# A decoder layer whose input arrives transposed: mean squares by narrow matmuls, and twelve early blocks of the embedding product

## The chip, the core and the metric

The kernel runs on one core of one Trainium2 chip. The metric is the device time in microseconds (us). One execution was profiled; its views name the engines PE (TensorE), DVE (VectorE), ACT (ScalarE), POOL (GpSimd) and SP (SyncE, which issues all DMAs here).

## The reference

One decoder layer over x (1024 tokens by 1024 features), all in fp32:

```
h      = RMSNorm(x) * norm_mix_g
proj   = h @ w_in                     # q, k, v, z_a, gate-lowrank, four conv parts, g_a, g_c
y_a    = (headnorm(GLA(q, k, v, gk)) * silu(z_a)) @ w_branch_a
y_c    = (cb * causal_conv3(cc * xc)) * silu(z_c) @ w_branch_c
merged = sigmoid(g_a + b_ga) * y_a + sigmoid(g_c + b_gc) * y_c
x1     = x + merged @ w_out
x2     = x1 + sigmoid(RMSNorm(x1) @ w_ple_gate) * (p @ w_ple_proj)
out    = RMSNorm(x2)
```

The change touches the first line, and the product p @ w_ple_proj, whose two factors (1024 by 256 and 256 by 1024) are called p and W_pe here.

## The kernel before

**Arithmetic.** Every large product is made of fp32r matmuls on a split of each operand: `hi` is a cast (ACT) and `lo` is the operand less `hi` (DVE), function `split`, line 546. `mm3` (line 557) issues three matmuls, hi by hi, hi by lo, lo by hi. The large products use a Strassen-like scheme with seven products of half-size blocks: class `Cell` (line 661) is one output cell, and `hres[k]` is the split block k of the transposed h that product k needs. Blocks 0 and 3 come from the first 512 tokens alone; 1, 2, 4, 5 and 6 are sums and differences with the second 512.

**Order.** Nothing is issued when the code calls it. A recorder (`Flow`, line 237) notes each operation with an assumed cost; `set_dues` (line 330) works out by when each is due; `put_in_order` (line 374) simulates five engines and writes one fixed order for each. Matmuls noted with `nc.side = False` keep their order; those with `nc.side = True` are put among them as soon as the simulation says that they could run. In it a load is over 2.2 us (`LATE`, line 466) behind the end of its bytes at 340 KB per us. On the chip each engine and SP's queue work that order off and wait at the first instruction whose operand isn't there. Buffers are kept by tag and count: SBUF tag `T` has four, the PSUM banks are `m0` to `m5`, and two more banks have the tag `o`.

**The first stage** (`prep0`, lines 838 to 930). Sixteen matmuls on zeros (line 834) come first. SP loads the first 512 columns of W_pe and of p (512 KB each, line 847), `vec`, four blocks of x of 128 tokens (512 KB each), the second columns of W_pe and p, and the other four blocks of x. `pe_block` (line 880) makes one 128 by 512 block of p @ W_pe by six matmuls in bank m4 or m5, ACT copies it out and SP stores it to DRAM, to be read near the end of the kernel. Eight blocks have their place ahead of h, eight are side work. `prep_x` (line 867) takes one block of x: ACT squares it and sums each row (`junk` holds the squares, nobody reads them), POOL makes mean + EPS and its power -0.5, DVE scales the rows, PE transposes eight 128 by 128 pieces into two `o` banks, and DVE multiplies them by `gmix` into the four tiles `hq` (transposed h by quarters). `two_products` (line 897) then runs products 0 and 3 of the four cells of g_a, and later of g_c, in banks m0 to m3, and `step(k)` builds `hres[k]`.

**After it** come the products v, q, k (phase `v`, line 935, begins with v0's product 0), the attention, the convolution, the merge and the two last products, none of which the change edits.

Of the kernel before, what the change touches and what calls it, by code (L numbers as in the profile page):

```python
# [9 lines left out]
F32 = mybir.dt.float32  # L10
# [226 lines left out]
class Flow:  # L237
# [136 lines left out]
    def put_in_order(self):  # L374
# [28 lines left out]
        while len(order) < len(ops):  # L403
            best = None
            for e in range(5):
                found = [(max(clock[e], w), n) for n in waiting[e] for w in [since(ops[n])] if w is not None]
                first = None
                if e == PE and at < len(main) and not ops[main[at]].left:
                    w = since(ops[main[at]])
                    if w is not None:  # L410
                        first = (max(clock[e], w), main[at])
                when = min([w for w, _ in found + ([first] if first else [])], default=None)
                if when is None or best and best[0] <= when:
                    continue
                ripe = [n for w, n in found if w <= when]
                pick = min(ripe, key=lambda n: (ops[n].due + (6.0 if ops[n].table and ops[n].table != table else 0.0), n),
                           default=None)
                best = (when, e, first[1] if pick is None else pick)
            assert best, "nothing can run"
            when, e, n = best  # L420
            o = ops[n]
            o.start = when
            if e == PE and not o.side:
                at += 1
            else:
                waiting[e].discard(n)
            cost = o.cost
            if o.table and o.table != table:
                cost, table = cost + 1.3, o.table
            clock[e] = when + cost  # L430
            if e == SP:
                pipe = max(pipe, when + 1.6) + o.bytes / 340e3
            for s in o.succs:
                q = ops[s]
                q.ready = max(q.ready, (pipe + LATE if e == SP else when + cost + q.preds[n])
                              + (SIDE if q.engine == PE != e and q.side else 0.0))
                q.left -= 1
                if not q.left and (q.engine != PE or q.side):
                    waiting[q.engine].add(s)
            for b in o.bufs:  # L440
                if b.place is None:
                    b.place = min((w, k) for k, w in enumerate(b.tag.free) if w is not None)[1]
                    b.tag.free[b.place] = None
                    b.tag.next += 1
                b.left -= 1
                if b.pool.name == "ps":
                    b.ends[e] = when + cost
                b.until = max(b.until, pipe + LATE if e == SP else when + cost + (0.0 if e == PE and not o.side else o.lat))
                if not b.left:
                    b.tag.free[b.place] = b.until  # L450
            order.append(o)
# [12 lines left out]
SIDE = 0.5  # L464
BACKLOG = 3.0
LATE = 2.2


@with_exitstack
def kernel(  # L470
# [6 lines left out]
    wgk2: bass.AP,  # L477
    wpe: bass.AP,
    pT: bass.AP,
    vecs: bass.AP,  # L480
    gbc: bass.AP,
    tri: bass.AP,
# [8 lines left out]
    def f(ap):  # L491
        return ap.bitcast(F32)
# [18 lines left out]
    vec = cp.tile([P, 62], F32, name="vec")  # L511
    dcs = cp.tile([P, H, 2, NP, 2], F32, name="dcs")
    dds = cp.tile([P, H, 2, NP], F32, name="dds")
    junk = cp.tile([P, D], BF16, name="junk")
    bgk = vec[:, 0:4]
    bga = vec[:, 4:12]
    bgc = vec[:, 12:20]
# [311 lines left out]
    hres = [None] * 7  # L829
    zero = bp.tile([P, 512], F32R, tag="u2", name="zero", bufs=2)  # L830
    nc.vector.memset(f(zero), 0.0)
    warm = [psm.tile([P, 512], F32, tag=f"m{i}", name=f"warm{i}") for i in range(6)]
    nc.side = False
    for n in range(16):
        mm(warm[n % 6], zero[:, 0:P], zero, start=True, stop=True)
    nc.side = True

    with phase("prep0") as pool:
        pr_ = slot(4, "h", "pTraw", (2, SEQ), F32)
        wr_ = slot(4, "l", "wperaw", (2, D), F32)  # L840
        xs = [slot(1 + n // 2, "hl"[n % 2], f"x0_{n}", (2, D), F32) for n in range(4)]
        xt = [xs[st // 2][:, st % 2, :] for st in range(8)]
        halves = [slice(hh * 512, (hh + 1) * 512) for hh in range(2)]
        pre = [Cell(f"{m}{c}p", "B", W[f"{m}{c}"], hres, gate_cons(c, bias, dst), prods=(0, 3))
               for m, bias, dst in (("ga", bga, gad), ("gc", bgc, gcd)) for c in range(4)]

        load(wr_[:, :, halves[0]], wpe[:, :, halves[0]])
        load(pr_[:, :, halves[0]], pT[:, :, halves[0]])
        load(vec, vecs)
        for st in range(4):  # L850
            load(xt[st], x[rows(st), :])
        load(wr_[:, :, halves[1]], wpe[:, :, halves[1]])
        load(pr_[:, :, halves[1]], pT[:, :, halves[1]])
        for st in range(4, 8):
            load(xt[st], x[rows(st), :])
        load(trim, tri)
        pth, ptl = slot(5, "h", "pThi", (2, SEQ)), slot(5, "l", "pTlo", (2, SEQ))
        wph, wpl = slot(6, "h", "wpehi", (2, D)), slot(6, "l", "wpelo", (2, D))

        def split_half(hi, lo, src, hh):  # L860
            cs = halves[hh]
            split(hi[:, :, cs], lo[:, :, cs], src[:, :, cs])

        q = [pool.tile([P, 4, HALF], F32, name=f"hq{i}") for i in range(4)]
        quad = {(0, 0): q[0], (1, 0): q[1], (1, 1): q[2], (0, 1): q[3]}

        def prep_x(st):
            ms = sm.tile([P, 1], F32, tag="ms", name=f"ms_x{st}", bufs=4)
            act(junk, xt[st], AF.Square, scale=1.0 / 32.0, accum_out=ms)
            r = rstd_of(ms, f"r_x{st}")  # L870
            nc.vector.tensor_scalar(xt[st], xt[st], r[:, 0:1], None, op0=ALU.mult)
            for kh in range(2):
                pt = pso.tile([P, 4, P], F32, tag="o", name=f"pt_x{st}_{kh}", bufs=2)
                for k in range(4):
                    kk = 4 * kh + k
                    transpose(pt[:, k, :], xt[st][:, kk * P:(kk + 1) * P])
                tt(quad[st // 4, kh][:, :, (st % 4) * P:(st % 4 + 1) * P], pt,
                   gmix[:, 4 * kh:4 * kh + 4, None].to_broadcast([P, 4, P]), op=ALU.mult)

        def pe_block(b, c):  # L880
            acc = psm.tile([P, 512], F32, tag=f"m{4 + (b + c) % 2}", name=f"pe{b}_{c}")
            nc.side = b >= 4
            for kt in range(2):
                mm3(acc, pth[:, kt, rows(b)], ptl[:, kt, rows(b)], wph[:, kt, halves[c]],
                    wpl[:, kt, halves[c]], kt == 0, kt == 1)
            nc.side = True
            t = bp.tile([P, 512], F32, tag="T", name=f"pe{b}_{c}", bufs=4)
            nc.scalar.copy(t, acc)
            store(ped[b][:, halves[c]], t)

        hb, steps = build_a("h", q)

        def step(k):
            steps[k]()
            hres[k] = hb[k]

        def two_products(cells):
            acc = [psm.tile([P, 512], F32, tag=f"m{n}", name=f"{c.name}X") for n, c in enumerate(cells)]
            for c, X in zip(cells, acc):
                c.product(0, X, True)  # L900
                t = ev(f"{c.name}s1")
                nc.scalar.copy(t, X)
                store(s1d[pre.index(c)], t)
            for c, X in zip(cells, acc):
                c.product(3, X, False)
                c.cons(0, 0, X)

        split_half(wph, wpl, wr_, 0)
        split_half(pth, ptl, pr_, 0)
        split_half(wph, wpl, wr_, 1)  # L910
        for c in range(2):
            for b in range(4):
                pe_block(b, c)
        for st in range(4):
            prep_x(st)
        step(0)
        step(3)
        split_half(pth, ptl, pr_, 1)
        for st in range(4, 8):
            prep_x(st)  # L920
        two_products(pre[:4])
        for k in (1, 2):
            step(k)
        two_products(pre[4:])
        step(4)
        for c in range(2):
            for b in range(4, 8):
                pe_block(b, c)
        step(6)
        step(5)  # L930

# [548 lines left out]
def _lay_out(inp):  # L1480
# [17 lines left out]
    def quads(m):  # L1498
# [15 lines left out]
        "wgk2": np.concatenate([a["w_gk2"][0]] * 8),  # L1514
        "wpe": a["w_ple_proj"][0].reshape(2, 128, 1024).transpose(1, 0, 2),
        "pT": a["p"][0, 0].T.reshape(2, 128, 1024).transpose(1, 0, 2),
        "vecs": vecs,
        "gbc": np.broadcast_to(a["norm_final_g"], (128, 1024)),
        "tri": np.triu(np.ones((128, 128), np.int32)),
# [21 lines left out]
```

## Time and profile before

| what | value |
|---|---|
| three runs, us | 1123.02, 1125.8, 1123.91 |
| their median, us | 1123.91 |
| the profiled execution, us | 1124.92 |
| its span, first to last instruction, us | 1123.1 |
| mean granted TensorE clock | 0.997 |

A row of the timeline has the start in us from the span's beginning, the length in us, the engine, the line (459 is the planner's one call, so operations are told apart by their tiles), the instruction, output<-inputs, partitions x elements, and the count of merged instructions; in brackets stands the idle time ahead of it and what ended it. `PEld` is PE's load of the stationary operand. A row of one tile's instructions has the count and the shortest, median and longest duration in ns, then the first and last start. In the table of stretches the numbers behind a stretch's length are busy us with the count of instructions for PE, PEld, DVE, ACT and POOL, then the granted clock, the DMA engines' busy share, and GB/s.

### The profile page before, as it was taken

To read this page: it belongs to the slowest core of one execution; us is meant where nothing else is said; L and a number is where in the kernel's file an instruction comes from. 1 tells how busy PE (TensorE), PEld (TensorE's weight loads), DVE (VectorE), ACT (ScalarE), POOL (GpSimd) and SP (SyncE) were. 2 spreads that over 40 slices of the span, in tenths; PEclk is the share of its full clock that TensorE was granted. 3 is DMA by queue.
4 is the path that set the end of the run, shared out by engine and by line. 5 is a ranking of instruction groups with operands and counts; after the bars stand their busy time and mean duration, and the time that the engine had idled before them with its cause. 6 is when DMAs were issued, how large, how long until landed. Compare 5 with 4: busy or idle time off the path is not lost. (4 is left out here: it accounts for less than half of the span.)

```text
span 1123.1 us, 15414 instructions
## 1 busy us (share of the span) xinstructions
PE 1104.9 (98%) x5132; PEld 915.3 (81%) x5132; DVE 858.3 (76%) x1370; ACT 585.4 (52%) x1089; POOL 72.2 (6%) x131
## 2 busy tenths in 40 slices
PE   8999999999999999999999999999999999999996
PEld 7788888888888888888888888888888887787884
DVE  6986776988785856757748677776999879879675
ACT  7766765654443333333343376766736444457553
POOL 1200000000000000000000022220000000102031
PEclk9999999999999999999999999999999999999998
DMA  9844466987993122121212599998594888787853
GB/s 345 273 169 142 133 194 190 276 237 264 318 328 126 57 86 65 55 94 46 94 56 69 192 292 307 348 294 293 207 317 162 288 260 291 274 273 267 285 192 126
DMA packets 154207, 232.66 MB, mean 207 GB/s; under 512 B 12304, under 2 KB 74000, under 8 KB 151056
## 3 DMA queue, kind: packets, MB, share of 16 engines
q1 hardware_dynamic: 154128, 231.68, 62.1%
q8 instruction: 40, 0.66, 0.2%
q14 instruction: 39, 0.32, 0.1%
HBM read 154.04 MB, written 77.59 MB: 206 GB/s over the span
## 5 line engine op out<-in xcount | busy, mean ns | idle before, releaser
L459 ACT ACTIVATE junk<-x 128x512 bf16<-128x512 f32 (+1 forms) x40 | 28.6, 716 | 23.5 <-DVE x L459 19.1
L459 POOL MEMSET t<- 128x2 f32 x8 | 0.8, 100 | 471.5 <-DVE u L459 271.0
L459 POOL TENSOR_SCALAR rg<-ms 128x1 f32<-128x1 f32 x8 | 8.0, 1003 | 260.9 <-ACT junk L459 260.9
L459 DVE TENSOR_TENSOR wt<-wt 128x512 f32<-128x512 f32 x32 | 21.8, 686 | 2.1 <-DMA szd<-sz 0.8
L459 DVE SCALAR_TENSOR_TENSOR u<-t,vec,u 128x1024 f32<-128x1024 f32 x16 | 20.5, 1278 | 0.0
L459 POOL TENSOR_TENSOR or<-or,mhalf 128x1 f32<-128x1 f32 x32 | 19.7, 618 | 2.6
L459 DVE COPY_PREDICATED aT<-trim,X 128x128 f32<-128x128 int32 x32 | 9.6, 300 | 11.0 <-PE X L459 8.3
L459 ACT ACTIVATE og<-op,or 128x256 f32<-128x256 f32 x32 | 15.1, 472 | 5.1 <-POOL or L459 3.6
L459 POOL TENSOR_SCALAR or<-oms 128x1 f32<-128x1 f32 x32 | 9.8, 305 | 124.1 <-ACT junk L459 123.9
L459 DVE TENSOR_TENSOR oT<-op,szl 128x256 f32<-128x256 f32 x32 | 13.4, 420 | 5.6 <-ACT junk L459 2.9
L459 DVE TENSOR_TENSOR vlo<-pt_v,vhi 128x512 fp32r<-128x512 f32 x16 | 11.0, 687 | 7.0 <-ACT vhi L459 6.9
L459 ACT ACT_TABLE_LOAD x12 | 15.4, 1283 | 0.9 <-PEq L1530 0.7
L459 ACT ACTIVATE junk<-op 128x256 bf16<-128x256 f32 x32 | 12.2, 382 | 6.9 <-PE op L459 6.2
L459 PE MATMUL op<-Sh,qkl 128*128 128x256 f32 x56 | 14.7, 283 | 0.0
L459 POOL TENSOR_SCALAR rf<-ms 128x1 f32<-128x1 f32 x8 | 10.4, 1295 | 65.3 <-ACT junk L459 65.2
L459 ACT CAST vhi<-pt_v 128x512 fp32r<-128x512 f32 x16 | 9.2, 584 | 9.7 <-PE pt_v L459 8.5
L459 PE MATMUL pe<-wpehi,pThi 128*128 128x512 f32 x32 | 13.3, 415 | 0.7 <-ACT pe L459 0.7
L459 PE MATMUL op<-vl,aTh 128*128 128x256 f32 x64 | 13.9, 290 | 0.0
L459 DVE SCALAR_TENSOR_TENSOR x<-x,rf,gfin 128x1024 f32<-128x1024 f32 x8 | 10.3, 1282 | 4.2 <-POOL rf L459 4.2
L459 ACT CAST aTh<-aT 128x128 fp32r<-128x128 f32 x32 | 9.5, 297 | 7.2 <-DVE aT L459 6.9
L459 DVE TENSOR_TENSOR Sl<-S,Sh 128x256 fp32r<-128x256 f32 x28 | 11.8, 421 | 1.6 <-ACT Sh L459 1.3
L459 PE MATMUL pe<-wpehi,pTlo 128*128 128x512 f32 x32 | 12.9, 404 | 0.0
(3213 smaller groups left out, 4191.8 us busy)
## 6 DMA issues: line engine op xcount, KB each, us to landing
qkl<-qkd SPq DMA_DIRECT2D x32, 320.0 KB, 5.0
x<-in_x_dram SPq DMA_DIRECT2D x16, 512.0 KB, 5.9
wt<-in_wb_dram SPq DMA_DIRECT2D x8, 1024.0 KB, 7.7
wtd<-wt SPq DMA_DIRECT2D x32, 256.0 KB, 4.7
vl<-vd SPq DMA_DIRECT2D x32, 256.0 KB, 5.0
uq<-ud SPq DMA_DIRECT2D x5, 1024.0 KB, 5.2
oq<-od SPq DMA_DIRECT2D x5, 1024.0 KB, 6.7
ped<-pe SPq DMA_DIRECT2D x16, 256.0 KB, 3.1
```

What stands on the lines that cost most here:

```text
L459: o.call(*[place(a) for a in o.args], **{k: place(a) for k, a in o.kw.items()})
```

## The change

The host also hands over x transposed (`xT`, 128 x 8 x 1024). It is loaded straight into the four `hq` tiles, in loads of two 128-feature pieces by 512 tokens (512 KB). Nothing is transposed but the reciprocal root: `scale_h(i)`, for each 512 tokens, squares the eight pieces on ACT, adds them up pairwise on DVE, sums over the features by eight fp32 matmuls against a column of ones (two for each 128 tokens), adds EPS on DVE, takes the power on POOL for four columns at once, spreads it over 128 columns on DVE, transposes that by four PE transposes, and scales the eight pieces on DVE by `gmix` and the transposed root.

The sixteen warm-up matmuls are seven. p and W_pe are loaded in pieces of 256 KB and split piece by piece; the two second-column pieces of W_pe now come ahead of x. Twelve blocks of p @ W_pe have their place ahead of h (tokens 0 to 511 by both column halves, tokens 512 to 1023 by the first), over banks m0 to m5 in turn; the first four run all their first halves of the contraction, then the second ones. Blocks of odd number are copied out by DVE instead of ACT. Four blocks remain as side work. In the simulation a load issued in its first 30 us is over 0.8 us behind its bytes instead of 2.2.

```diff
-                q.ready = max(q.ready, (pipe + LATE if e == SP else when + cost + q.preds[n])
+                q.ready = max(q.ready, (pipe + (LATE if when > START else 0.8) if e == SP else when + cost + q.preds[n])
...
+START = 30.0
...
-    junk = cp.tile([P, D], BF16, name="junk")
+    junk = cp.tile([P, 512], BF16, name="junk")
...
-    for n in range(16):
+    for n in range(7):
         mm(warm[n % 6], zero[:, 0:P], zero, start=True, stop=True)
...
+        def get_x(i):
+            for n in (0, 3) if i == 0 else (1, 2):
+                for kp in range(0, 4, 2):
+                    kk = 4 * quad[n][1] + kp
+                    load(q[n][:, kp:kp + 2, :], xT[:, kk:kk + 2, halves[i]])
+
+        for kt in range(2):
+            load(pr_[:, kt, halves[0]], pT[:, kt, halves[0]])
+            load(wr_[:, kt, halves[0]], wpe[:, kt, halves[0]])
+        for kt in range(2):
+            load(wr_[:, kt, halves[1]], wpe[:, kt, halves[1]])
+        get_x(0)
+        load(vec, vecs)
+        for kt in range(2):
+            load(pr_[:, kt, halves[1]], pT[:, kt, halves[1]])
+        get_x(1)
...
+        def scale_h(i):
+            both = (0, 3) if i == 0 else (1, 2)
+            acc = slot(1, "hl"[i], f"sq{i}", (4, 512), F32)
+            for j, (n, kp) in enumerate((n, kp) for n in both for kp in (0, 2)):
+                d = acc[:, 0:2, :] if j == 0 else acc[:, 2:4, :] if j % 2 else slot(2, "hl"[i], f"sr{i}", (4, 512), F32)[:, 0:2, :]
+                act(d, q[n][:, kp:kp + 2, :], AF.Square, scale=1.0 / 32.0)
+                if j:
+                    tt(acc[:, 0:2, :], acc[:, 0:2, :], d, op=ALU.add)
+            sums = pso.tile([P, 4, P], F32, tag="o", name=f"ms{i}", bufs=2)
+            for s in range(4):
+                for kt in range(2):
+                    mm(sums[:, s, 0:1], acc[:, kt, s * P:(s + 1) * P], ones, start=kt == 0, stop=kt == 1)
+            r = sm.tile([P, 4], F32, tag="rx", name=f"r_x{i}", bufs=2)
+            nc.vector.tensor_scalar(r, sums[:, :, 0], EPS, None, op0=ALU.add)
+            nc.gpsimd.tensor_tensor(r, r, mhalf[:, 0:1].to_broadcast([P, 4]), op=ALU.pow)
+            rb = bp.tile([P, 4, P], F32, tag="u2", name=f"rb{i}", bufs=2)
+            nc.vector.tensor_copy(rb, r[:, :, None].to_broadcast([P, 4, P]))
+            rt = pso.tile([P, 4, P], F32, tag="o", name=f"rt{i}", bufs=2)
+            for s in range(4):
+                transpose(rt[:, s, :], rb[:, s, :])
+            rt = rt.rearrange("p s t -> p (s t)")
+            for n in both:
+                for k in range(4):
+                    kk = 4 * quad[n][1] + k
+                    stt(q[n][:, k, :], q[n][:, k, :], gmix[:, kk:kk + 1], rt, op0=ALU.mult, op1=ALU.mult)
+
+        BANKS = (0, 1, 2, 3, 4, 5, 0, 1, 2, 3, 4, 5)
+
+        def pe_blocks(bs, c, by_kt=False):
...
+                nc.side = at[0] > len(BANKS)
...
+                    (nc.vector.tensor_copy if b % 2 else nc.scalar.copy)(t, acc[b - bs[0]])
+                    store(ped[b][:, halves[c]], t)
...
-        split_half(wph, wpl, wr_, 0)
-        split_half(pth, ptl, pr_, 0)
+        for kt in range(2):
+            split(pth[:, kt, halves[0]], ptl[:, kt, halves[0]], pr_[:, kt, halves[0]])
+            split(wph[:, kt, halves[0]], wpl[:, kt, halves[0]], wr_[:, kt, halves[0]])
+        pe_blocks(range(0, 4), 0, True)
         split_half(wph, wpl, wr_, 1)
-        for c in range(2):
-            for b in range(4):
-                pe_block(b, c)
-        for st in range(4):
-            prep_x(st)
+        pe_blocks(range(0, 4), 1)
+        split_half(pth, ptl, pr_, 1)
+        pe_blocks(range(4, 8), 0)
+        scale_h(0)
         step(0)
         step(3)
-        split_half(pth, ptl, pr_, 1)
-        for st in range(4, 8):
-            prep_x(st)
         two_products(pre[:4])
+        scale_h(1)
         for k in (1, 2):
             step(k)
         two_products(pre[4:])
         step(4)
-        for c in range(2):
-            for b in range(4, 8):
-                pe_block(b, c)
+        pe_blocks(range(4, 8), 1)
         step(6)
         step(5)
```

More of the change, by code (lines that the diff above doesn't have):

```diff
@@ L447, in put_in_order @@
                     b.ends[e] = when + cost
-                b.until = max(b.until, pipe + LATE if e == SP else when + cost + (0.0 if e == PE and not o.side else o.lat))
+                b.until = max(b.until, pipe + (LATE if when > START else 0.8) if e == SP else when + cost + (0.0 if e == PE and not o.side else o.lat))
                 if not b.left:
@@ L479 @@
     pT: bass.AP,
+    xT: bass.AP,
     vecs: bass.AP,
@@ L831 @@
     nc.vector.memset(f(zero), 0.0)
+    ones = sm.tile([P, 1], F32, name="ones")
+    nc.gpsimd.memset(ones, 1.0)
     warm = [psm.tile([P, 512], F32, tag=f"m{i}", name=f"warm{i}") for i in range(6)]
     nc.side = False
-    for n in range(16):
+    for n in range(7):
         mm(warm[n % 6], zero[:, 0:P], zero, start=True, stop=True)
@@ L840 @@
         wr_ = slot(4, "l", "wperaw", (2, D), F32)
-        xs = [slot(1 + n // 2, "hl"[n % 2], f"x0_{n}", (2, D), F32) for n in range(4)]
-        xt = [xs[st // 2][:, st % 2, :] for st in range(8)]
         halves = [slice(hh * 512, (hh + 1) * 512) for hh in range(2)]
@@ L845 @@
                for m, bias, dst in (("ga", bga, gad), ("gc", bgc, gcd)) for c in range(4)]
-        load(wr_[:, :, halves[0]], wpe[:, :, halves[0]])
-        load(pr_[:, :, halves[0]], pT[:, :, halves[0]])
-        load(vec, vecs)
-        for st in range(4):
-            load(xt[st], x[rows(st), :])
-        load(wr_[:, :, halves[1]], wpe[:, :, halves[1]])
-        load(pr_[:, :, halves[1]], pT[:, :, halves[1]])
-        for st in range(4, 8):
-            load(xt[st], x[rows(st), :])
-        load(trim, tri)
+        q = [pool.tile([P, 4, HALF], F32, name=f"hq{i}") for i in range(4)]
@@ L857 @@
+        quad = [(0, 0), (1, 0), (1, 1), (0, 1)]
         pth, ptl = slot(5, "h", "pThi", (2, SEQ)), slot(5, "l", "pTlo", (2, SEQ))
         wph, wpl = slot(6, "h", "wpehi", (2, D)), slot(6, "l", "wpelo", (2, D))
-        def split_half(hi, lo, src, hh):
[L861 to L873, printed above, removed]
-                for k in range(4):
[L875 to L884, printed above, removed]
-                    wpl[:, kt, halves[c]], kt == 0, kt == 1)
[L886 to L889, printed above, removed]
+        def get_x(i):
[3 more added lines that the diff above has]
+                    load(q[n][:, kp:kp + 2, :], xT[:, kk:kk + 2, halves[i]])
@@ new lines @@
+        for kt in range(2):
[8 more added lines that the diff above has]
+        get_x(1)
+        load(trim, tri)
+        def split_half(hi, lo, src, hh):
+            for kt in range(2):
+                cs = halves[hh]
+                split(hi[:, kt, cs], lo[:, kt, cs], src[:, kt, cs])
@@ new lines @@
+        at = [0]
+        BANKS = (0, 1, 2, 3, 4, 5, 0, 1, 2, 3, 4, 5)
+        def pe_blocks(bs, c, by_kt=False):
+            acc = []
+            for b in bs:
+                n = BANKS[at[0]] if at[0] < len(BANKS) else 4 + at[0] % 2
+                acc.append(psm.tile([P, 512], F32, tag=f"m{n}", name=f"pe{b}_{c}"))
+                at[0] += 1
+            todo = [(b, kt) for kt in range(2) for b in bs] if by_kt else [(b, kt) for b in bs for kt in range(2)]
+            for b, kt in todo:
+                nc.side = at[0] > len(BANKS)
+                mm3(acc[b - bs[0]], pth[:, kt, rows(b)], ptl[:, kt, rows(b)], wph[:, kt, halves[c]],
+                    wpl[:, kt, halves[c]], kt == 0, kt == 1)
+                nc.side = True
+                if kt == 1:
+                    t = bp.tile([P, 512], F32, tag="T", name=f"pe{b}_{c}", bufs=4)
+                    (nc.vector.tensor_copy if b % 2 else nc.scalar.copy)(t, acc[b - bs[0]])
+                    store(ped[b][:, halves[c]], t)
@@ L906, in two_products @@
                 c.cons(0, 0, X)
-        split_half(wph, wpl, wr_, 0)
-        split_half(pth, ptl, pr_, 0)
+        for kt in range(2):
+            split(pth[:, kt, halves[0]], ptl[:, kt, halves[0]], pr_[:, kt, halves[0]])
+            split(wph[:, kt, halves[0]], wpl[:, kt, halves[0]], wr_[:, kt, halves[0]])
+        pe_blocks(range(0, 4), 0, True)
         split_half(wph, wpl, wr_, 1)
-        for c in range(2):
-            for b in range(4):
-                pe_block(b, c)
-        for st in range(4):
-            prep_x(st)
+        pe_blocks(range(0, 4), 1)
+        split_half(pth, ptl, pr_, 1)
+        pe_blocks(range(4, 8), 0)
+        scale_h(0)
         step(0)
         step(3)
-        split_half(pth, ptl, pr_, 1)
-        for st in range(4, 8):
-            prep_x(st)
         two_products(pre[:4])
+        scale_h(1)
         for k in (1, 2):
@@ L1516, in _lay_out @@
         "pT": a["p"][0, 0].T.reshape(2, 128, 1024).transpose(1, 0, 2),
+        "xT": a["x"][0].T.reshape(8, 128, 1024).transpose(1, 0, 2),
         "vecs": vecs,
```

## The prediction

> **What bounds the kernel now.** The first part of the profile, the busy time of each engine, says who is the bound; the table of stretches then says where that engine is not full.
>
> ```profile
> span 1123.1 us, 15414 instructions
> PE 1104.9 (98%) x5132; PEld 915.3 (81%) x5132; DVE 858.3 (76%) x1370; ACT 585.4 (52%) x1089; POOL 72.2 (6%) x131
> ```
> ```profile
> 0.00:100.00 100.00, 96.38 (x435) 77.33 (x436) 75.41 (x105) 70.78 (x115) 13.12 (x25) 1.00 0.68 236
> 100.00:200.00 100.00, 100.00 (x470) 82.05 (x469) 71.87 (x112) 60.04 (x97) 0.00 (x0) 1.00 0.59 179
> 1000.00:1123.10 123.10, 110.15 (x500) 90.32 (x498) 93.96 (x132) 66.00 (x124) 23.10 (x24) 0.97 0.65 226
> ```
>
> PE is the first number behind each stretch's length. It has a matmul running 98% of the span, all of 100 to 200 us, and its only large holes are in the last 123 us, which the change leaves alone. So the time is PE's list of matmuls plus its holes, and a microsecond won or lost before 100 us is carried to the end, since PE works its list off in order. The question is what the first 60 us of PE hold. Its waits up to 130 us, and its timeline, whose first column is the start:
>
> ```profile
> PE ga0pX L459 <- DVE h0lo L459: 0.8, 1, 0.8
> PE pe L459 <- ACT pe L459: 0.7, 1, 0.7
> PE pt_x L459 <- DVE hq L459: 0.6, 1, 0.6
> ```
> ```profile
> 8.02 0.39 PE L459 MATMUL pe<-wpehi,pThi 128*128 128x512 f32 x1
> 8.25 0.39 PE L459 MATMUL pe<-wpelo,pThi 128*128 128x512 f32 x1
> ...
> 10.65 0.39 PE L459 MATMUL pe<-wpehi,pTlo 128*128 128x512 f32 x1
> 11.73 0.50 PE L459 MATMUL pe<-wpehi,pThi 128*128 128x512 f32 x1 [0.70 <-ACT pe L459]
> ...
> 14.06 1.03 PE L459 MATMUL pt_x<-ident,x 128*128 128x128 f32 x8
> 14.85 0.48 PE L459 MATMUL pe<-wpehi,pThi 128*128 128x512 f32 x1
> 15.16 0.40 PE L459 MATMUL pe<-wpelo,pThi 128*128 128x512 f32 x1
> ...
> 23.86 0.39 PE L459 MATMUL ga0pX<-h0hi,ga0phi 128*128 128x512 f32 x1
> 25.09 0.50 PE L459 MATMUL ga0pX<-h0lo,ga0phi 128*128 128x512 f32 x1 [0.84 <-DVE h0lo L459]
> ...
> 32.07 0.39 PE L459 MATMUL ga2pX<-h0lo,ga2phi 128*128 128x512 f32 x1
> 32.52 1.07 PE L459 MATMUL pt_x<-ident,x 128*128 128x128 f32 x8
> ...
> 33.89 0.40 PE L459 MATMUL ga2pX<-h0lo,ga2phi 128*128 128x512 f32 x1
> 34.84 0.66 PE L459 MATMUL pt_x<-ident,x 128*128 128x128 f32 x4 [0.56 <-DVE hq L459]
> ```
>
> Starts are read, not durations, because matmuls overlap: 8.02 to 8.25 is 0.23 us a matmul. So four things can be won: the real work begins at 8.02; eight transposes of x cost 14.85 - 14.06 = 0.79 and another 0.08 at the change back (15.16 - 14.85 - 0.23), 0.87 in all, so the 64 cost about 6.9; and the holes are 0.85 (10.88 to 11.73), 1.0 (24.09 to 25.09), 0.2 (32.30 to 32.52) and 0.7 (34.12 to 34.84), 2.8 together.
>
> **The change part by part.** *The start.* What has to arrive first, and x's first half:
>
> ```profile
> 4.65 1.04 ACT L459 CAST wpehi<-wperaw 128x1024 fp32r<-128x1024 f32 x1 [2.65 <-DMA wperaw<-in_wpe_dram]
> ...
> 6.11 1.04 ACT L459 CAST pThi<-pTraw 128x1024 fp32r<-128x1024 f32 x1 [0.42 <-DMA pTraw<-in_pT_dram]
> ```
> ```profile
> 4.94 0.94 SPq L459 DMA_DIRECT2D x<-in_x_dram  x1
> ...
> 8.74 0.33 SPq L459 DMA_DIRECT2D ga2praw<-in_wc_dram  x1
> ```
> ```profile
> DMA to landing us min/median/max: 5.3/6.7/9.1
> ```
> ```profile
> L459 DVE TENSOR_TENSOR wpelo<-wperaw,wpehi x2: 1226/1226/1227, 5.7 to 9.8; 128x1024 fp32r<-128x1024 f32 x2
> L459 DVE TENSOR_TENSOR ga0plo<-ga0praw,ga0phi x2: 680/684/687, 17.8 to 23.2; 128x512 fp32r<-128x512 f32 x2
> L459 DVE TENSOR_SCALAR x<-x,r_x x8: 745/750/756, 12.2 to 40.5; 128x1024 f32<-128x1024 f32 x8
> L459 DVE TENSOR_TENSOR hq<-pt_x,vec x16: 679/684/692, 14.7 to 43.6; 128x512 f32<-128x512 f32 x16
> ```
>
> Half a megabyte lands every 1.46 us (4.65, 6.11), so quarters land near 3.9 and 4.65. ACT then casts w's quarter (about 0.55, half of 1.04) until 5.25, DVE takes 0.68 for the remainder: PE runs steadily from about 6.05. That is -2.0. The four extra load issues cost SP 0.33 each; SP reaches the fourth x load near 5 us, as now (4.94), behind the same 1.5 MB of p and W and 1.5 MB of x, so I let it land as now, at 4.94 + 9.1 = 14.0. The planner's new 0.8 behind a load is no work; it puts the first half megabyte at 0.72 + 1.6 + 1.54 + 0.8 = 4.66 against 4.65 above, so I price it at nothing.
>
> *The clock.* Nine warm-up matmuls go.
>
> ```profile
> L459 PE MATMUL warm<-zero x16: 395/628/796, 1.4 to 7.8; 128*128 128x512 f32 x16
> ```
>
> Sixteen starts from 1.4 to 7.8 are 0.42 us apart on the mean, near double the 0.23 of the work behind them: PE runs at half pace for about its first 6 us, though the granted clock reads 1.00. Seven end near 4.6, and 6.05 comes after more than a microsecond with hardly a matmul. If the 6 us count from 1.4 all the same, PE is slow until 7.3 and loses half of 1.25, 0.6; if they count anew, until 12, and it loses 3.0. The stream is broken, so I take a value nearer the upper end: +2.0.
>
> The Trainium skill, "TensorE: Matmul & The Clock Gate", Part 1, speaks against the change here: the gate opens only after a busy window of about 3.4 us whose phase is not tied to the kernel, so a gap can spoil a window. An estimate by that page alone is a loss of 1.7 to 3.4 us, and a sum of -4.3 to -2.6 instead of the -4.0 below; the slow first 6 us agree with it, and no row here shows a gap before the clock is up.
>
> *The sums.* 64 transposes go (-6.9), 8 of the broadcast root come (+0.9). Sixteen narrow fp32 matmuls are added. The nearest row is the fp32 score product: line 1190 issues it 32 times and the trace holds 64, two passes each.
>
> ```profile
> 646.08 0.39 PE L459 MATMUL ga1Y<-h2hi,ga1lo 128*128 128x512 f32 x1
> 646.31 0.38 PE L459 MATMUL X<-qkl 128*128 128x128 f32 x2
> 646.53 0.27 PE L459 MATMUL X<-ident,qkl 128*128 128x128 f32 x1
> ```
>
> Two passes take 0.22, so 32 take 3.5, and 3.6 with the changes to and fro. Below, the loads of weights set a floor by the transposes' pace (0.79 / 8 = 0.10, 3.2); above, a full matmul's 0.23 would give 7.4. I take 3.6, since the score product also loads 128 fp32 columns per pass.
>
> *The holes.* The 0.85 goes: six banks and an alternation of ACT and DVE replace two banks behind one ACT copy. The 0.2 and 0.7 stood at x's transposes. The 1.0 before h0 depends on who is later. PE: 6.05, 72 matmuls x 0.23 = 16.6, half the sums 1.8, four transposes 0.5, clock 2.0: 26.9. The chain to h0: x at 14.0, its Square 1.06, an add 1.23, eight sums 1.8, the root, its broadcast about 0.7, transposes 0.4, two scalings 1.3, cast 1.04, remainder 1.23, and some 1.2 for nine handovers. The root is POOL's:
>
> ```profile
> L459 POOL TENSOR_SCALAR r_x<-ms_x x8: 221/461/3433, 11.3 to 38.0; 128x1 f32<-128x1 f32 x8
> L459 POOL TENSOR_TENSOR r_x<-r_x,mhalf x8: 567/567/901, 11.6 to 38.8; 128x1 f32<-128x1 f32 x8
> ```
>
> One pow of one column takes 0.57; four columns lie between 0.57 and 2.3, and I take 0.6. The chain then ends near 24.6, two microseconds ahead of PE. So -2.8 of old holes, and +1.2 of new ones for the second half's sums and transposes, which stand in PE's fixed order among the gate products, and for h0's second chunk. The bounds for the new ones are 0 and the rivals below.
>
> *The rest.* DVE loses eight scalings (8 x 0.75) and gains six adds (6 x 1.23), eight copies out of PSUM (about 0.68 each, by the row from pt_x) and two small steps a half (1.8): +8.6. The sixteen scalings that replace the reads of pt_x have the same shape. ACT loses those copies and eight accumulator reads. This hides: the last remainder of h, and the first product that needs any of the later ones, stand far apart.
>
> ```profile
> 65.08 2.36 DVE L459 TENSOR_TENSOR h6lo<-hq,h6hi 128x1024 fp32r<-128x1024 f32 x2
> ```
> ```profile
> L459 PE MATMUL v0X<-h0hi,v0hi x4: 389/389/389, 89.1 to 91.1; 128*128 128x512 f32 x4
> ```
>
> From 67 to 89 us there are 22 us of cover; were it gone, at most 8.6 would show. Four more blocks' stores (1 MB) fall before h0, and SP holds each until its copy is done; what stands behind them on SP is second-half x and gate weights, which have until 26 us. The shorter junk tile costs nothing.
>
> Sum: -2.0 - 6.9 + 0.9 + 3.6 + 2.0 - 2.8 + 1.2 = -4.0 us. Against the profiled execution (1124.92, a span of 1123.1 and 1.8 around it) that is 1120.9; that execution lies 1.0 above the median of 1123.91, against which it is 1119.9.
>
> **The rivals.** *The clock is up early and the chain never shows.* Cold loss 0.6 and no new hole: -6.6, 1117.3. For it: the planner's order gives the chain two microseconds. Against it: the gap after seven warm-up matmuls.
>
> *The narrow matmuls cost a full matmul's pace per pass*: 3.8 more, -0.2, 1123.7. Against it: 0.11 a pass in the score product.
>
> *The root is late.* POOL's 3.43 above is a step of 0.22 that could not finish while DVE ran one two-input subtraction after another; the pow has DVE's splits beside it too. With 2.9 on each half and x's last quarter 2 us later behind gate weights, h0 is ready at 29.5, PE waits 2.6 there and 2.9 in the second half, in place of 1.2: +0.3, 1124.2. "SBUF — State Buffer" of the Trainium skill, in "Who interferes with whom", gives this as a lock: a DVE instruction with two SBUF inputs shuts out a GpSimd one that reads SBUF; the 3.43 agrees.
>
> *Slower: PE stands in its own fixed order behind the chain.* The sums and the root's transposes are put among matmuls that could run. If POOL is shut out (2.9) and DVE also has a queue of splits and copies before broadcast and scaling (three at 0.68, 2.0), each half is 4.9 late at PE: 9.8 in place of 1.2, +4.6, 1128.5. It is slower by over 0.3% from 4.3 us of lateness per half. For it: before h0 DVE has eight splits, six copies, four scalings and two gate remainders at 0.68, three adds and a remainder at 1.23, some 18.5 us of work between 5 and 26 us. Against it: the slow clock delays PE by 2.0 and the chain by nothing.
>
> *The clock counts anew after the gap*: a loss of 3.0 instead of 2.0, -3.0, 1120.9. For it: no row shows the pace rising over a gap. Against it: the gap is short beside the 6 us. The page on the clock gate above has this rule, with a window in place of a count.
>
> *The quarters land no sooner than the halves*, so the work starts near 7 instead of 6.05: -3.0, 1120.9. Against it: the landings above are in proportion to the bytes.
>
> **How the numbers follow.** A measurement of this kernel can tell about 0.3%, 3.4 us, from no change; the marks are 1120.5 and 1127.3. My case, between -5.5 and -3.4, 0.38; early clock 0.17; clock anew 0.10, late root 0.11, expensive sums 0.08 and late quarters 0.05, all between -3.4 and +3.4, together 0.34; slower 0.11. So faster 0.55, same 0.34, slower 0.11. The likeliest gives 1119.9. The range reaches from 1116.0, just below the early clock, to 1124.6, a little over the late root; the slower case and a little at the lower end stay out.
>
> **What would show it.** Right: the first pe matmul before 6.2; matmuls 0.42 apart until 9 to 12 us; two passes of about 0.11 per narrow matmul; h0's first product at 26 to 28 us with under 0.5 us of wait; v0's first product 4 us earlier than 89.1. Wrong: a wait of PE at rt, ms or h0lo of over 2 us; a POOL pow of over 2 us; holes past 60 us that the kernel did not have.

## The result, and the profile after

The changed kernel takes 1139.91 us (median of four, 1138.01 to 1143.24) against 1124.4 of the kernel before beside it. The ratio is 1.0131, 95% interval 1.0110 to 1.0151: **slower by 15.5 us**, where 4.0 us less was forecast. The profiled execution is the one of 1143.24.

The head of its page, to set beside the same two lines of before:

```profile
span 1141.5 us, 15326 instructions
PE 1123.5 (98%) x5099; PEld 917.4 (80%) x5099; DVE 868.9 (76%) x1384; ACT 581.2 (51%) x1077; POOL 60.8 (5%) x118
```

PE has 33 matmuls fewer (5099 against 5132), is as full as before (98%), and yet its busy time has grown by 18.6 us. So it does not wait longer; the same matmuls take longer. The table of stretches, PE alone, shows where. First before, then after:

```profile
200.00:400.00 200.00, 200.00 (x884) 1.00 0.69 223
400.00:600.00 200.00, 200.00 (x884) 1.00 0.23 73
```
```profile
10.00:20.00 10.00, 7.29 (x25) 0.80 1.04 381
20.00:30.00 10.00, 10.00 (x36) 0.51 0.54 160
30.00:40.00 10.00, 10.00 (x46) 1.00 0.75 278
...
200.00:400.00 200.00, 200.00 (x866) 1.00 0.70 225
400.00:600.00 200.00, 200.00 (x865) 1.00 0.21 69
```

Behind PE's count stand the granted clock, the DMA share and GB/s. Between 400 and 600 us PE is full in both kernels, both have the whole clock, and the DMA engines are four fifths idle; still 865 matmuls fit in where 884 did. No line of that stage was edited. From the starts in the trace: between 250 and 600 us one 128x512 matmul follows the other after 226.67 ns before (always 226 or 227) and after 231.59 ns now (224 to 237). Over the whole program some 4,290 such steps (those under 0.3 us), 4.2 ns longer on the mean, are **18 us**.

The second thing is in the first 30 us of PE's timeline after:

```profile
1.44 3.35 PE L459 MATMUL warm<-zero 128*128 128x512 f32 x7 [1.44 <-DVE zero L459]
5.36 0.79 PE L459 MATMUL pe<-wpehi,pThi 128*128 128x512 f32 x1 [0.57 <-ACT pThi L459]
5.95 0.63 PE L459 MATMUL pe<-wpelo,pThi 128*128 128x512 f32 x1
...
8.94 0.55 PE L459 MATMUL pe<-wpehi,pTlo 128*128 128x512 f32 x1
9.33 0.40 PE L459 MATMUL pe<-wpehi,pThi 128*128 128x512 f32 x1
9.56 0.39 PE L459 MATMUL pe<-wpelo,pThi 128*128 128x512 f32 x1
...
13.19 0.39 PE L459 MATMUL pe<-wpehi,pTlo 128*128 128x512 f32 x1
15.12 0.50 PE L459 MATMUL pe<-wpehi,pThi 128*128 128x512 f32 x1 [1.54 <-ACT wpehi L459]
16.79 0.80 PE L459 MATMUL pe<-wpelo,pThi 128*128 128x512 f32 x1 [1.16 <-DVE wpelo L459]
17.38 0.63 PE L459 MATMUL pe<-wpehi,pTlo 128*128 128x512 f32 x1
17.80 0.63 PE L459 MATMUL pe<-wpehi,pThi 128*128 128x512 f32 x1
...
29.33 0.81 PE L459 MATMUL rt<-ident,rb 128*128 128x128 f32 x4
29.89 0.48 PE L459 MATMUL pe<-wpelo,pThi 128*128 128x512 f32 x1
```

Real work begins at 5.36 and is steady from 5.95. The steps are 0.43 us until 9.3 and 0.23 from there: the clock is up. At 13.19 PE runs out of work, because W_pe's second columns are not there; a wait of 1.54 for their cast and one of 1.16 for their remainder follow, and behind them the steps are 0.43 again until 29.7 (the granted clock of 20 to 30 us is 0.51): 12.9 us at half pace, 6.4 us lost in this execution. The others fared better: four executions have 1143.2, 1141.4, 1138.0 and 1138.4 us at mean clocks of 0.991, 0.993, 0.996 and 0.996. From the rise at 9.3 to the rise at 29.7 are 20.4 us. The Trainium skill, "TensorE: Matmul & The Clock Gate", Part 1, has the clock set by windows of about 3.4 us that run free of the kernel. 20.4 is 6.0 of them, so the trace agrees, as far as one interval can.

Why the work was not there, SP's issues behind the first one of p and the first two of W_pe tell (start, length):

```profile
2.10 0.43 SPq L459 DMA_DIRECT2D pTraw<-in_pT_dram  x1
2.57 0.43 SPq L459 DMA_DIRECT2D hq<-in_xT_dram  x1
3.05 0.47 SPq L459 DMA_DIRECT2D wperaw<-in_wpe_dram  x1
3.56 0.95 SPq L459 DMA_DIRECT2D hq<-in_xT_dram  x2
4.55 1.13 SPq L459 DMA_DIRECT2D wperaw<-in_wpe_dram  x1
```

The code notes the two second-column pieces of W_pe ahead of x. The planner, which sends the load that is due first, put half a megabyte of x ahead of the first piece and another megabyte ahead of the second.

What the first reading could not show is the cause of the slower steps. One candidate is not in any view: **the memory that the program gives its tiles**. The edit adds a tile of 4 bytes (`ones`), moves `mhalf` in the order of first use, and replaces eight small tiles of x's rows (32 bytes each, so 256 together) by two. In the built program every split operand of a matmul, the fourteen residents (`h`, `u`, `o`, ...) and the sixteen tiles of the weight ring (`whi`, `wlo`), starts at 160 past a multiple of 256 bytes before the change, by the accident that the small tiles between them come to 256 bytes. After it, residents start at 160, 192 or 224 past, and of the ring fourteen tiles at 224 and two at 192. Below, the place of a tile is this remainder of its start address by 256 bytes. In these products a resident is the moving operand, whose 512 columns go through PE, and a tile of the ring is the stationary one, which PE loads ahead.

### The profile page after: what moved, and what is told of

The parts are those of the page before. It is cut to its first block, busy times and chain, and to the rows that moved or that the text cites. A ratio compares the mean times of both kernels' runs of the same rounds, so it can differ in the third digit from the quotient of the medians.

```text
span 1141.5 us, 15326 instructions
## 1 busy us (share of the span) xinstructions
PE 1123.5 (98%) x5099; PEld 917.4 (80%) x5099; DVE 868.9 (76%) x1384; ACT 581.2 (51%) x1077; POOL 60.8 (5%) x118
## 5 line engine op out<-in xcount | busy, mean ns | idle before, releaser
L459 ACT ACTIVATE junk<-x 128x512 bf16<-128x512 f32 x32 | 20.1, 629 | 22.5 <-DVE x L459 18.4
L459 DVE COPY_PREDICATED aT<-trim,X 128x128 f32<-128x128 int32 x32 | 9.6, 300 | 10.6 <-PE X L459 8.1
L459 PE MATMUL pe<-wpelo,pThi 128*128 128x512 f32 x32 | 15.3, 477 | 1.2 <-DVE wpelo L459 1.2
L459 PEld LDWEIGHTS X<-qkl 128*128 128x128 f32 x64 | 11.3, 188 | 2.5 <-DMA qkl<-qkd 0.7
```

The lines of the kernel that those rows point to most:

```text
L459: o.call(*[place(a) for a in o.args], **{k: place(a) for k, a in o.kw.items()})
```

## The experiments

Theory A: the step from one matmul to the next goes by the start addresses of its operands. Theory B, the rival: it comes from the new order, the banks, the transposed load or the DMAs. Beside these, theory C on the start: the two pieces of W_pe behind x cost their waits and the clock. When the first four were written I took the grain of A to be 64 bytes; that was wrong. Each ratio below is to the kernel before, run beside that experiment; across experiments the ratios compare better than the times.

**Whole 64-byte steps for every tile, and a mixture put into the kernel before.**

```diff
-        b = Buffer(self, self.tags[tag], size, dtype, name or tag)
+        b = Buffer(self, self.tags[tag], -(-size // 16) * 16, dtype, name or tag)
```

The first is the changed kernel with this line.

> The changed kernel with every small tile rounded up to 64 bytes, so that all tiles start at a multiple of 64 bytes; nothing else differs. Theory A (addresses): the changed kernel's extra 4- and 16-byte tiles put the operands of the matmuls at two different offsets within 64 bytes (0 and 32), and matmul starts went from 227 to 231 ns apart for it; here the pace is 227 ns again and the time is 1118 to 1124 us. Rival B (the pace follows from the new order of work or from traffic): pace stays at 231 ns, time 1138 to 1143 us. Rival C (the loss lies in the first 40 us, in PE's waits and slow clock): time also stays at 1138 to 1143 us, since those are not touched.

Measured: 1138.16 us, ratio 1.0115 (1.0093 to 1.0138), steps of 231.9 ns. Nothing gained. The operands were at 0 and at 64 past 256 now, one resident at 192. The second is the kernel before with two residents 32 bytes longer, which leaves 160, 192 and 224:

```diff
-        b = Buffer(self, self.tags[tag], size, dtype, name or tag)
+        b = Buffer(self, self.tags[tag], size + (8 if tag in ("r6l", "r0h") else 0), dtype, name or tag)
```

> The kernel before, with two resident tiles (W_pe's remainder, later block 6, and block 0's cast) 32 bytes longer, so that of the matmul operands some start at 0 and some at 32 within 64 bytes; all work and its order are that of before. Theory A (addresses): pace 230 to 233 ns instead of 227, time 1137 to 1147 us. Rivals B and C: no change, 1123 to 1126 us.

Measured: 1144.12 us, ratio 1.0178 (1.0154 to 1.0201). Its table of stretches, PE alone:

```profile
200.00:400.00 200.00, 200.00 (x864) 1.00 0.69 226
400.00:600.00 200.00, 200.00 (x864) 1.00 0.20 69
```

The old order, banks and loads, and the new pace: 64 bytes of memory alone cost 20 us. So theory B is not needed for a slow pace; that it has no part in the changed kernel's is shown by the run with one place, below. The grain of 64 fell in the run ahead of this one. A third kept all residents at a multiple of 64 and the ring 32 past one, by 32 bytes more behind ten tiles, so that places within 256 bytes were mixed among both (the smallest tiles are left out of the 64-byte steps here):

```diff
+EXTRA = {'raw_2': 8, 'raw_8': 8, 'raw_9': 8, 'whi_4': 8, 'r0l_0': 8, 'whi_7': 8, 'r3h_0': 8, 'wlo_3': 8, 'r3l_0': 8, 'wlo_7': 8}
...
+            self.size += EXTRA.get(spot, 0)
```

> The changed kernel with all moving operands (the residents) at 0 within 64 bytes and all stationary ones (the ring of hi and lo pieces) at 32. Theory A1 (the two operands of a matmul must share the offset): pace 231 ns or more, time 1135 to 1145 us. Theory A2 (each stream must keep its own offset from matmul to matmul, whatever the other has): pace 227 ns, 1118 to 1124 us.

Measured: 1143.55 us, ratio 1.0170 (1.0142 to 1.0198), 232.7 ns: slow too. What before had and none of these had is one and the same place within 256 bytes for all.

**W_pe's pieces at the head of SP's queue**, in the kernel with 64-byte steps:

```diff
             load(wr_[:, kt, halves[1]], wpe[:, kt, halves[1]])
+            nc.early.append(nc.ops[-1])
...
+        for o in self.early:
+            o.due = -1e3
```

> The changed kernel with 64-byte tiles, and the two second-column pieces of W_pe issued as early as they can be, ahead of x. Theory: in the changed kernel PE idled 3.1 us for these pieces (13.4 to 16.8 us) and the clock fell back to half until 29.7; with them early the idle goes, the clock stays up, and the time is 2 to 6 us below that of the run with 64-byte tiles alone, 1114 to 1119 us. Rival: x, which then lands later, takes it back at the sums (PE waits at ms or at rt): within 1 us of the run with 64-byte tiles alone.

Measured: 1139.95 us, 1.0133 (1.0114 to 1.0152), no gain. The due time was too early: both pieces went ahead of p's first columns, and PE's waits became

```profile
PE pe L461 <- ACT pThi L461: 3.4, 1, 3.4
...
PE ga0pX L461 <- DVE h0lo L461: 1.2, 1, 1.2
```

The wait was moved, not removed; the run says nothing on theory C.

**One place in 256 bytes.** The changed kernel with two of its small tiles at 256 bytes: with `ones` at 32, every resident and every tile of the ring is at 160 again.

```diff
-        b = Buffer(self, self.tags[tag], size, dtype, name or tag)
+        b = Buffer(self, self.tags[tag], 64 if tag in ("mhalf", "rx") else size, dtype, name or tag)
```

> The changed kernel, with two small tiles (the -0.5 of the root and the two of the scales) enlarged to 256 bytes, so that every resident factor and every tile of the ring starts 160 bytes past a multiple of 256 again, as in the kernel before; order and work as in the changed kernel. Theory (the pace of the matmuls goes by the start addresses of both operands, and is best where all share one place in 256 bytes): pace from 231.6 back to 226.7 ns between 250 and 600 us, 4394 x 4.2 ns = 18.5 us less than the changed kernel, 1121 us, and less where the clock's fall in the start stage does not happen. Rival (the pace comes from the new order, the fewer banks or the transposed load, and addresses play a part only in the other test): 231 ns and 1140 us as changed.

Measured: **1119.65 us**, ratio to before 0.9951 (0.9933 to 0.9968).

```profile
10.00:20.00 10.00, 6.93 (x26) 0.83 1.06 399
20.00:30.00 10.00, 10.00 (x52) 1.00 0.77 253
...
200.00:400.00 200.00, 200.00 (x884) 1.00 0.68 220
400.00:600.00 200.00, 200.00 (x884) 1.00 0.23 71
```

884 matmuls again, 226.67 ns, and 20.3 us less than the changed kernel, of which 18.5 are the steps (4,290 times 4.3 ns). All 5099 matmuls come in the same order in both kernels, and banks and loads are kept, so theory B has nothing left to explain. The clock, for the rest, fell for 3.4 us in this execution instead of 12.9 (0.83 in the second ten us, 1.00 in the third).

The same with 128 bytes instead of 256, so that operands stand at 32 or at 160:

```diff
-        b = Buffer(self, self.tags[tag], 64 if tag in ("mhalf", "rx") else size, dtype, name or tag)
+        b = Buffer(self, self.tags[tag], 32 if tag in ("mhalf", "rx") else size, dtype, name or tag)
```

> As the kernel with the same addresses, but the small tiles enlarged to 128 bytes instead of 256: the operands start at 32 or at 160 past a multiple of 256 (two thirds at 32), all at 32 past a multiple of 128. If places are told apart within 128 bytes: 226.7 ns and the same time as with equal places. If within 256: some 230 ns or more and 12 to 18 us slower than with equal places.

Measured: 1132.51 us, 1.0072 (1.0051 to 1.0092), 230.25 ns. A shared place in 128 bytes does not do. One in 256 does: in the kernel ahead of this one the operands still lie at 1696, 1952, 160 and 416 past a multiple of 2048.

**Which difference counts: between the two operands, or from one matmul to the next?** For this the memory was set out on purpose: all residents first, then the ring, then the rest. The start was taken from the kernel with W_pe first (below).

```diff
+    def lay(self, order):
...
+        resident = [b for b in spots if b.tag.name[0] == "r" and b.tag.name[1].isdigit()]
+        ring = [b for b in spots if b.tag.name in ("whi", "wlo")]
+        for group, lead in ((resident, 0), (ring, 0)):
+            if lead:
+                group[0].pool.opened().tile([P, lead], F32, tag="lead" + group[0].tag.name, name="lead", bufs=1)
+            for b in group:
+                b.get()
...
-            for o in self.put_in_order():
+            order = self.put_in_order()
+            self.lay(order)
+            for o in order:
```

> As the kernel with the same addresses and W_pe's loads ahead of x, but the memory is set out on purpose: first the fourteen residents, then the sixteen tiles of the ring, all at 128 past a multiple of 256 (a multiple of 64), the rest behind them. Theory (only that the two operands share a place in 256 bytes counts): 226.7 ns between 250 and 600 us, 1118 us as there. Rival (160 is a place of its own, or the neighbours in memory matter): 229 ns or more, 1128 us or more.

Measured: 1118.63 us, 0.9917 (0.9895 to 0.9939), 226.67 ns: 128 is as good a place as 160. Then the ring was moved as a whole, by 128 bytes, with as much less for `mhalf`, so that most tiles behind stay put; and in the same way by 64 (16 and 48 in place of 32 and 32) and by 32 (8 and 56):

```diff
-        for group, lead in ((resident, 0), (ring, 0)):
+        for group, lead in ((resident, 0), (ring, 32)):
...
-        b = Buffer(self, self.tags[tag], 64 if tag in ("mhalf", "rx") else size, dtype, name or tag)
+        b = Buffer(self, self.tags[tag], 32 if tag == "mhalf" else 64 if tag == "rx" else size, dtype, name or tag)
```

> As the kernel set out on purpose, with the sixteen tiles of the ring 128 bytes further on: residents all at 128 past a multiple of 256, ring all at 0, so that from one matmul to the next nothing changes place, but the two operands of each matmul stand 128 bytes apart. Theory (the operands of one matmul must share a place): 230 to 233 ns, 12 to 25 us slower than set out alike. Rival (only a change of place from one matmul to the next costs): 226.7 ns and no slower.

> The same with the ring 64 bytes further on (residents at 128, ring at 192). Theory (operands of one matmul must share a place): 230 to 233 ns. If the distance sets the price: less than at 128 bytes. Rival (only changes cost): 226.7 ns.

> The same with the ring 32 bytes further on (residents at 128, ring at 160), the distance that most products of the changed kernel have (192 and 224). Theory (operands of one matmul must share a place within 256 bytes, 32 bytes being enough to part them): 230 to 234 ns, 12 to 26 us slower than set out alike. Rival (32 bytes are one place, 64 or 128 are not): 226.7 ns, 1118 us.

Measured: 1139.71 us (1.0105, 1.0085 to 1.0124), 1144.17 (one execution) and 1142.96 (1.0161, 1.0144 to 1.0178). The table of stretches of the four, 400 to 600 us, set out alike first, then 128, 64 and 32 bytes apart:

```profile
400.00:600.00 200.00, 200.00 (x884) 1.00 0.21 71
```
```profile
400.00:600.00 200.00, 200.00 (x863) 1.00 0.21 70
```
```profile
400.00:600.00 200.00, 200.00 (x859) 1.00 0.21 70
```
```profile
400.00:600.00 200.00, 200.00 (x859) 1.00 0.21 70
```

The steps are 226.67, 232.38, 233.33 and 233.33 ns. In these three nothing changes place from one product to the next; only the moving operand (a resident) and the stationary one (a tile of the ring) differ. So it is the moving and the stationary operand that must share their place, and the price is 21 to 27 us here (1.0105 and 1.0161 against 0.9917; for the ring 64 bytes on, with its one execution, 1144.17 less 1118.63). Which stationary operand is open: PE loads the next matmul's while one runs (in the kernel with one place the matmul of 300.25 us is loaded from 300.02, when the one ahead of it starts), and with a ring at one place these runs can't tell a matmul's own from the next one's.

The traces of three kernels that mix places (the changed one, the one with 64-byte steps, the one with 128 bytes) bear this out inside one execution. The program's places, put beside the matmuls of 60 to 1000 us one by one, give the step where a matmul and six on each side are alike. Where all operands are at one place it is 226.9, 227.6 and 227.3 ns (159, 156 and 160 steps); where the two operands of none share a place, 232.5, 232.5 and 232.7. Where the two always share one, but it changes among the thirteen, it is 229.7, 228.4 and 227.7 (84, 78 and 78 steps): a change seems to cost something too, but no run was made for it. Why the hardware does this is not shown by these runs.

**The start.** Equal places, and the pieces of W_pe just behind the first four quarters:

```diff
+        n = self.early[0]
+        for o in self.ops[n:n + 2]:
+            o.due = max(q.due for q in self.ops[n - 4:n]) + 1e-3
...
+        nc.early = [len(nc.ops)]
         for kt in range(2):
             load(wr_[:, kt, halves[1]], wpe[:, kt, halves[1]])
```

> The same addresses, and the two loads of W_pe's second columns issued right behind the first four quarters, ahead of the first load of x. Theory (those two loads behind x hold TensorE 1.5 and 1.2 us, and these holes let the clock fall): no wait over 1 us at the pieces of W_pe, no fall of the clock behind 10 us, 3 to 10 us less than the kernel with the same addresses alone. Rival (x, 0.5 MB or 1.5 us later, then holds h's first product by as much): the same time within 1 us, with the wait at the split of h instead.

Measured: 1118.18 us, 0.9936 (0.9921 to 0.9951), 1.5 less than with equal places alone, where 3 to 10 were expected, and the two intervals overlap. PE's waits of the first 40 us, equal places alone and then with W_pe first:

```profile
PE pe L459 <- ACT wpehi L459: 1.9, 1, 1.9
PE warm L459 <- DVE zero L459: 1.4, 1, 1.4
PE pe L459 <- DVE wpelo L459: 1.2, 1, 1.2
PE pe L459 <- ACT pThi L459: 0.5, 1, 0.5
```
```profile
PE warm L462 <- DVE zero L462: 1.4, 1, 1.4
PE ga0pX L462 <- DVE h0lo L462: 0.9, 1, 0.9
PE ga0pX L462 <- ACT h0hi L462: 0.3, 1, 0.3
PE pe L462 <- ACT pThi L462: 0.2, 1, 0.2
```

The 3.1 us at W_pe are gone, 1.2 come at h instead, and the clock does not fall (1.00 in all stretches up to 1000 us). In the two profiled executions v0's first product starts 2.6 us earlier (78.3 against 80.9). The executions also lie closer: 1116.3 to 1118.9 at a mean clock of 0.997 in all six, against 1116.7 to 1124.5 at 0.990 to 0.997 in seven. So theory C holds in the profile for the waits, and the clocks speak for its other half; but its worth in time can't be told from nothing here. Nor do these waits always bring the clock down. In the profile of the run with 64-byte steps they are there too (1.0 and 1.2 us, the second ending at 15.32), and the clock stays up behind them:

```profile
10.00:20.00 10.00, 7.87 (x42) 1.00 1.06 403
20.00:30.00 10.00, 10.00 (x47) 1.00 0.92 305
```

With sixteen warm-up matmuls in place of seven on top of that:

```diff
-    for n in range(7):
+    for n in range(16):
         mm(warm[n % 6], zero[:, 0:P], zero, start=True, stop=True)
```

> As the kernel before this one, with the sixteen warm-up matmuls of the kernel before instead of seven. Theory (the cut warm-up brings the first product 2.0 us forward, and the clock goes by a grid of windows that more warm-up reaches no sooner): 2 us slower than with seven. Rival (seven leave the first window too empty, so that the clock comes up late or falls): the clock is up earlier, and 1 to 5 us faster than with seven.

Measured: 1117.4 us, 0.9930 (0.9916 to 0.9944): no difference from seven that can be told. Its timeline shows both sides:

```profile
1.44 5.64 PE L462 MATMUL warm<-zero 128*128 128x512 f32 x16 [1.44 <-DVE zero L462]
6.91 0.39 PE L462 MATMUL pe<-wpehi,pThi 128*128 128x512 f32 x1
7.14 0.39 PE L462 MATMUL pe<-wpelo,pThi 128*128 128x512 f32 x1
```

The first product is 1.9 us later than with seven (5.00), and v0's first product only 0.9 (79.2).

## Why the prediction was wrong, step by step

**The step that failed** is the one that carried the rest of the program over unchanged: "a microsecond won or lost before 100 us is carried to the end", with "The shorter junk tile costs nothing" and not a word on the other small tiles. The sum has a term for all that the edit issues and none for what it places. That term is +18 us of longer steps against the kernel before. Between the changed kernel and the one with equal places it is 18.5 of the 20.3 us in the medians; for the other 1.8 the clock is the likeliest cause, not shown by itself. None of the rivals had it; the sign that was named, holes past 60 us, did not come, since there are no holes: each step is 2% longer.

**With equal places the sum held.** That kernel is 5.6 us faster than the kernel before beside it (1119.65 against 1125.28), where -4.0 was forecast, and in the range. That it came so near is in part luck. In that kernel's profile the clock was up near 6.0, so the start lost some 0.1 in place of 2.0, but a second fall lost 1.7; the new hole took 3.1 in place of 1.2. With these the sum is -2.3, and some 2 us of what was measured are small steps that were not taken apart. Its first products at three points, q0 and gt3 before (v0's row of before stands in the prediction), then v0, q0 and gt3 with equal places:

```profile
L459 PE MATMUL q0X<-h0hi,q0hi x4: 387/389/396, 178.0 to 180.5; 128*128 128x512 f32 x4
```
```profile
L459 PE MATMUL gt3X<-wg0hi,gt3hi x4: 389/389/389, 1076.2 to 1078.3; 128*128 128x512 f32 x4
```
```profile
L459 PE MATMUL v0X<-h0hi,v0hi x4: 389/389/389, 80.9 to 82.9; 128*128 128x512 f32 x4
```
```profile
L459 PE MATMUL q0X<-h0hi,q0hi x4: 387/389/396, 173.7 to 176.2; 128*128 128x512 f32 x4
```
```profile
L459 PE MATMUL gt3X<-wg0hi,gt3hi x4: 389/389/389, 1071.2 to 1073.3; 128*128 128x512 f32 x4
```

v0's is 8.2 us earlier than 89.1, twice what was forecast, but 16 side matmuls of the gate's low rank (`lowp`, 3.6 us) that stood ahead of it before stand behind it now. By q0 this is evened out: 4.3 earlier, and 5.0 at the gate product near the end.

- *The start, -2.0, and the clock, +2.0.* The start was right (steady from 5.95, forecast 6.05). The clock was up at 9.3, inside the forecast's 7.3 to 12, and lost (9.3 - 5.95) / 2 = 1.7 there. Together they were priced at nothing, and nothing is what sixteen against seven gives. A second fall of the clock was not in the sum: 6.4 us in the profiled execution, 1.7 in the one with equal places.
- *The sums, +3.6.* Right. The first half, in the slow stretch, took 3.27 (20.79 to 24.06). At full clock:

```profile
52.12 1.84 PE L459 MATMUL ms<-ones,sq 128*128 128x1 f32 x16
53.82 0.48 PE L459 MATMUL ga2pX<-h3hi,ga2plo 128*128 128x512 f32 x1
```

  Sixteen passes take 53.82 - 52.12 = 1.70 us, 0.106 each, against 0.11; the rival at a full matmul's pace is out.
- *The holes, -2.8 and +1.2.* Old ones gone, but the new one is at W_pe's pieces, 2.7 to 3.1 us, and not at the second half's sums: I took the order of the code for the order of the queue.
- *The root, 0.6.* Too low but harmless:

```profile
L459 POOL TENSOR_TENSOR r_x<-r_x,mhalf x2: 1018/1027/1036, 24.6 to 54.2; 128x4 f32<-128x4 f32 x2
```

  Four columns take 1.03 us, inside the bounds of 0.57 and 2.3. The lock on POOL did not show, and no wait of PE at `rt` or `ms` either: the rivals "the root is late" and "slower" did not happen. The sign at h0 failed all the same: its first product, forecast for 26 to 28 us, starts at 35.2 in the changed kernel and at 29.6 with equal places, both without a wait, behind the holes at W_pe and the slow clock.
- *DVE, +8.6, hidden.* It is +10.6 (858.3 to 868.9), and PE has no wait between 40 and 110 us in the changed kernel. Right.

## What to carry to other kernels

Before a change of tiles is priced, write down where the built program puts the operands of the main matmuls, before and after: a tile of 4 bytes can shift all behind it, and here the two operands of a matmul at different places within 256 bytes made each step 2 to 3% longer, without a wait or a hole to see. The count of matmuls in a stretch where PE is full is the quickest test. And read the order of loads from SP's issues, not from the code, when a planner stands between them.

## What was not expected of the hardware

In these runs the step between fp32r matmuls of 128x512 is 226.67 ns when both operands start at the same place in 256 bytes, the same for all (160 or 128 past), 232.4 when they are 128 apart, and 233.3 when they are 64 or 32 apart. A place shared within 64 or 128 bytes alone doesn't help (231.9 and 230.3 ns). The kernel before had the good case by accident: the changed kernel is 1.3% slower than it, and the same kernel with two small tiles enlarged is 0.5% faster, 0.6% with W_pe's pieces ahead of x.
